# Experts' gate and up weights with eight consecutive feature rows on a partition

## The chip, the cores and the metric

The kernel runs on one core of a Trainium2 chip. The core has five engines that run side by side: TensorE (PE, with its weight loads shown apart as PEld), VectorE (DVE), ScalarE (ACT), GpSimd (POOL) and SyncE (SP), and 16 DMA engines that carry all transfers. The metric is the device time of one execution in microseconds. All times below are of the kernel before the change.

## What is computed

Two blocks work on 256 tokens of 1024 features, in float32. The first block (attention, a pool mixer and a gated feed-forward) is not touched. The second block has two layers, and each does this:

```python
mix = hybrid_mixer(x, ...)
x = layer_norm(ALPHA * x + mix, ln1_g[l], ln1_b[l])
ffn = grouped_moe(x, router_w, router_bias, w_gate[l], w_up[l], w_down[l])
x = layer_norm(ALPHA * x + ffn, ln2_g[l], ln2_b[l])
```

The experts' part, with 16 experts of 512 inner features, two of them chosen for a token:

```python
aff = jax.nn.sigmoid((xt @ router_w).astype(jnp.float32))
...
gates = jnp.sum(jax.nn.one_hot(e_idx, N_EXPERTS, dtype=jnp.float32) * wts[..., None], axis=1)
hg = jnp.einsum('nd,edf->nef', xt, w_gate)
hu = jnp.einsum('nd,edf->nef', xt, w_up)
act = jax.nn.silu(hg) * hu * gates[:, :, None].astype(hg.dtype)
out = jnp.einsum('nef,efd->nd', act, w_down)
```

The contraction of `w_gate` and `w_up` runs over the 1024 features of a token. Their order in it is free, as long as weights and tokens have the same one.

## The kernel before

The 1024 features are cut into 8 tiles of 128 (`KD`). A contraction over features puts 128 of them on the partitions at a time and adds up 8 such steps in PSUM. The tile framework orders the instructions of each engine by itself, within their dependencies and by its own estimate of when they can start, so the order of the code is not always the order on the engine.

At the start of the program SP issues the loads of x and of the first layer's weights `w_in`. POOL issues small loads on its own queue: in the code first `at` (constants of the attention) and the parts of `bw` (lines 266 to 275), then the tiles of the pool `const` (`upb`, `cr`, `rbias`, `rw`, lines 276 to 284).

In a layer of the second block the output projection leaves its sums in PSUM, 128 tokens a half. The first layer norm writes them as `z` (line 1075), tokens on partitions and the 1024 features next to each other, as 8 blocks of 128. TensorE transposes `z`, and `affine` (line 1083) scales the transposed tiles by the norm's gain and bias, a scalar for each partition, which gives `xp`. The router takes `xp`. Beside that, POOL splits `z` into a high and a low part, `zh` and `zl` (lines 1120 to 1122), since a product with both parts keeps float32's accuracy. VectorE works out the chosen experts in a chain of small steps (lines 1123 to 1151), and each token's slot of an expert (`sid`, line 1160); `residual` (line 1096) puts the scaled `xp` into PSUM, where the experts add to it.

`slots` (line 1165) turns the slots into a matrix `G` of zeros and ones for four experts. `gather` (line 1185) multiplies `zh` and `zl` with `G`, feature tile by feature tile, and `affine` scales the result to `xg`: features on partitions, 64 slots for each of four experts. `gate_up` (line 1201) contracts `xg` with the gate or the up weights of a pair of experts: feature tile `4 * h + k` of `xg` meets `W[..., k]` of half `h`. Each matmul takes 64 slots and 512 columns, in float32; the trace shows two records for each. The down products follow, and `combine` (line 1224) adds the outputs to the tokens. The stage runs over 8 pairs of experts.

`Experts.pump` (line 713) issues the weights on SP's queue in the order of their use, in pieces of 1 MB: four feature tiles of a gate or up matrix, or two of the four tiles of a down matrix. The first gate pieces and those of the last two pairs come in halves (lines 722 to 728 and 736 to 751). A piece goes to a ring or to tiles that earlier work has left, and SP waits until the space is free. Gate and up go by `"(k p) f -> p k f"`: a partition gets one row of 512 numbers from each feature tile, 2 KB at a time. Down goes by `"(p k) f -> p k f"`: a partition gets two consecutive rows of 1024 numbers, 8 KB in one run.

Of the kernel before, what the change touches and what calls it, by code (L numbers as in the profile page):

```python
# [10 lines left out]
F32 = mybir.dt.float32  # L11
# [10 lines left out]
KD = D // 128  # L22
# [8 lines left out]
# Scores of a head: 128 queries with 128 keys, then 128 queries with all 256 keys.  # L31
# [3 lines left out]
def body(tc, a, out, dbg=None, upto=None):  # L35
# [9 lines left out]
    def A(name, shape=(128, 512)):  # L45
        """One bank of PSUM."""
        return psum.tile(list(shape), F32, tag="A", name=name, bufs=4)

    def H(name, shape=(128, 2, 512)):
        """Two banks of PSUM."""  # L50
        return psum.tile(list(shape), F32, tag="H", name=name, bufs=2)
# [16 lines left out]
    def pin(i):  # L68
        """Keeps an instruction in the order of the program on its engine."""
        return tc.keep_in_program_order(i)  # L70

# [12 lines left out]
    def split(raw, shape=(1024,), eng=None, tile_=hl8, scale=1.0):  # L84
        """raw = hi + lo, both exact in float32r."""
        t = tile_("hl", F32R, (128, 2, 1024))
        n = int(np.prod(shape))
        hi, lo = (t[:, i, 0:n] for i in range(2))
        if len(shape) == 2:
            hi, lo = (v.rearrange("p (a b) -> p a b", b=shape[1]) for v in (hi, lo))  # L90
        if raw is not None:
            se.activation(hi, raw, AF.Copy, scale=scale)  # L92
            HI["lo"] = lo_of(lo, raw, hi, eng)
        return hi, lo

    HI = {}
    def keep_warm(n, dst):
        """Without work the clock of the tensor engine falls to half: this bridges a wait."""
        for _ in range(n):
            te.transpose(dst, ident, ident)  # L100
# [3 lines left out]
    def after(i, col):  # L104
        """behind[i] = 1, once col is there: keeps an operation scaled by it behind col."""
        ve.tensor_scalar(behind[:, i:i + 1], col, 1.0, 1.0, op0=ALU.max, op1=ALU.min)

    def table(func, col):
        """Loads the table of a function, once col is there."""
        se.activation(warm[:, 1:2], col, func, scale=0.0, bias=epsc[0:1, 0:1])  # L110

# [29 lines left out]
    # rows of per-channel vectors, put on partitions by the tensor engine  # L141
# [57 lines left out]
    def pre(seq, i, ahead=2, scale=1.0):  # L199
        """Keeps the splits of the units in seq up to i + ahead issued."""  # L200
        for name, j in seq[pre.done:i + ahead + 1]:
            HI[name, j] = split(W[name][:, j], scale=scale)
        pre.done = max(pre.done, min(i + ahead + 1, len(seq)))
# [47 lines left out]
    class at:  # L251
        """What only the attention needs (and the convolution, at first): a tile for each layer."""
# [27 lines left out]
    # the last rows come a second time, as the router takes 32 columns at once and drops 16  # L280
# [12 lines left out]
    def tm_mm(c, acc, k):  # L293
# [3 lines left out]
        if c == k == 0:  # L297
            # the low part of the weights comes last
            for i, (x, w) in enumerate(((hh, wh), (hl, wh), (hh, wl))):
                for tt in range(2):  # L300
                    for h in range(2):
                        tm_mm.last = mm(acc[tt][h], x[:, 0, tt * 128:(tt + 1) * 128], w[:, h * 512:h * 512 + 512], i == 0, False)
            return
# [15 lines left out]
    for k in range(KD):  # L319
# [4 lines left out]
        if k == 3:  # L324
            # statistics of the norm, and the vectors that come later
# [52 lines left out]
    def softmax_heads(S, n_, scale, nscale, values, hi, lo):  # L378
        """Scores of two heads, a bank each, to attention outputs with features on partitions."""
# [74 lines left out]
    def fm_out(units, xh, xl, evac, then=None):  # L454
        """8 feature tiles [128, 256] in 4 banks; units: (weight name, row) per contraction tile."""
# [101 lines left out]
    def up_split(i, ss=(0, 1)):  # L557
        """hi and lo of the weights of tile pair i, gate and value."""
        c, o = divmod(i, 2)
        for s in ss:  # L560
            UP[i, s] = split(W[f"up{c}{s}"][:, :, o * 128:o * 128 + 128], (KD, 128))
# [9 lines left out]
    def row_of(cols):  # L571
        """Two columns [128, 1] of tokens as a row [128, 256] on every partition."""
# [33 lines left out]
    def up_pair(i):  # L606
# [6 lines left out]
        # the first waits for the last of h2  # L613
# [59 lines left out]
    # =============================== second block ===============================  # L673
# [29 lines left out]
    class Experts:  # L703
        """The experts' weights in 8 KB pieces, which go around the ring and the tiles
        that the attention has left."""

        def __init__(self, l):
            self.l, self.n, self.final = l, 0, []
            self.todo = [(p, m, h, e) for p in range(8) for m in range(3) for h in range(2) for e in range(2)]
            # the second half of the first gate's contraction goes to the ring, which has space later  # L710
            self.todo[2:10] = self.todo[4:10] + self.todo[2:4]

        def pump(self, n):
            while self.n < min(n, len(self.todo)):
# [4 lines left out]
                if p == m == 0:  # L719
                    # the first in halves, as the space of the first halves is needed early  # L720
                    self.n += 2
                    for b in range(2):
                        for e in range(2):
                            t = ring.tile([128, 2, 512], F32, name=name)
                            c0 = 512 * h + 256 * b
                            sy.dma_start(t, a["w_gate_2"][self.l, e, c0:c0 + 256].rearrange("(k p) f -> p k f", p=128))
# [8 lines left out]
                src = src.rearrange("(k p) f -> p k f" if m < 2 else "(p k) f -> p k f", p=128)[:, shape[1] * h:shape[1] * (h + 1)]  # L735
                if p < 6:
                    sy.dma_start(t, src)
                elif p == 7 and m == 2:
                    # all first halves of the columns, then all second
# [5 lines left out]
                elif e:  # L745
                    # in halves, so that the products don't wait long for any and little is left after the last
# [9 lines left out]
    def transpose_rows(z, evac, one_bank):  # L756
        """z(k, tt) [128 tokens, 128 features] -> features on partitions."""
# [32 lines left out]
    def layer(l, xT, xh, xl, general=False):  # L790
# [7 lines left out]
        # high, high and low part of a head's index queries below each other, high, low and high of the keys  # L798
# [3 lines left out]
        # high and low part of a head's queries below each other, the keys' high parts twice and their low parts  # L802
        dq2, dk2 = act("dq2", F32R, (128, 8, T)), t2("dk2", (128, 2, T), F32R)
        nh, nl = act("nh", F32R), act("nl", F32R)
        # queries and keys, a head a column block: 64 rows without position, then the rope
        # q_r * cos, q_r * sin on the side of the queries, the rotated key and its swapped halves on the keys'
# [27 lines left out]
        def proj(i, ahead=1):  # L834
            for q in range(ahead + 1):
                prep(i + q)
            if i not in PS:
                # the first two side by side, as x comes slower than one of them takes it
# [49 lines left out]
        def index_scores(g):  # L888
# [4 lines left out]
            for b, h in enumerate(hs):  # L893
                # all keys for both halves of the queries; the second half's scores go over the first's of later keys
# [30 lines left out]
        def latent_stats():  # L925
            """1 / rms of the latent queries and keys, a token a partition; that of the keys as a row too."""
# [44 lines left out]
        def queries(g):  # L971
            """Two heads: columns without position, and the rope's columns twice."""
# [21 lines left out]
        def dsa_pair(j):  # L994
            S = H("sc")
            for tt, (c, n) in enumerate(SPAN):
                t_ = slice(tt * 128, tt * 128 + 128)
                for i in range(2):
                    h = 2 * j + i
                    r = slice(32 * (h % 4), 32 * (h % 4) + 2)  # L1000
                    # all keys for both halves of the queries; the second half's scores go over the first's of later keys
# [81 lines left out]
        def affine(dst, src, k, eng):  # L1083
            g, b = V(f"ln1g{l}", k), V(f"ln1b{l}", k)
# [11 lines left out]
        def residual():  # L1096
            """The scaled residual in PSUM, where the experts add to it."""
# [22 lines left out]
        for tt in range(2):  # L1120
            ge.tensor_copy(zh[:, tt], z[:, tt])
            lo_of(zl[:, tt], z[:, tt], zh[:, tt], ge)
        ve.tensor_tensor(out=bia, in0=aff, in1=rbias[:, None, :].to_broadcast([128, 2, 16]), op=ALU.add)
        b4 = R[:, 1].rearrange("p (g e) -> p g e", e=4)
        # the two best of a group of four sum to the best of: both of a pair, the better of each pair
# [33 lines left out]
        # a token's slot of an expert counts from 1, and 0 is none  # L1159
        ve.scalar_tensor_tensor(out=sid, in0=pk, scalar=1.0, in1=sel, op0=ALU.add, op1=ALU.mult)  # L1160

# [1 line left out]
        XG, GS, Y, S6 = {}, {}, {}, {}  # L1163

        def slots(q):
            """Which token has which of the 64 slots of four experts, and the slots' gates."""
# [18 lines left out]
        def gather(q, bs=range(4)):  # L1185
            """The tokens of four experts, features on partitions, 64 slots each."""
# [4 lines left out]
            for b in bs:  # L1191
# [6 lines left out]
                for i in range(2):  # L1198
                    affine(xg[:, 2 * b + i], pg[:, i], 2 * b + i, (se, ve)[b % 2])
# [16 lines left out]
        def slot_rows(p):  # L1216
            """The slots of two experts as rows."""
# [13 lines left out]
        def dense_experts():  # L1231
            """Every expert over every token."""
# [176 lines left out]
    if dbg is None:  # L1409
        # More tokens for an expert than it has slots: the second block again, in the general way.  # L1410
# [14 lines left out]
def constants():  # L1425
# [24 lines left out]
    # rows 0 to 31: which of the key's 32 features comes first, which second  # L1450
# [50 lines left out]
```

## Time and profile before

| | |
|---|---|
| device time, median of 3 runs | 1088.08 us (1087.83 to 1089.63) |
| span of the profiled execution, first to last instruction | 1082.4 us |
| PE busy | 1034.8 us (96%) |
| DVE busy | 540.0 us (50%) |
| ACT busy | 427.3 us (39%) |
| POOL busy | 80.4 us (7%) |
| DMA | 295.08 MB, mean 273 GB/s |
| loads of the experts' gate weights | 40 of 1024 KB, 48 of 512 KB |
| loads of the experts' up weights | 48 of 1024 KB, 32 of 512 KB |
| loads of the experts' down weights | 48 of 1024 KB, 32 of 512 KB |

The span runs from the first to the last instruction of the one execution that was profiled; the device time has what lies around it as well, 5.7 us at the median. A busy share says how long an engine worked, not whether others waited for it. That is read from the waits and from the order of time.

### The profile page before, as it was taken

To read this page: it belongs to the slowest core of one execution; us is meant where nothing else is said; L and a number is where in the kernel's file an instruction comes from. 1 tells how busy PE (TensorE), PEld (TensorE's weight loads), DVE (VectorE), ACT (ScalarE), POOL (GpSimd) and SP (SyncE) were. 2 spreads that over 40 slices of the span, in tenths; PEclk is the share of its full clock that TensorE was granted. 3 is DMA by queue.
4 is the path that set the end of the run, shared out by engine and by line. 5 is a ranking of instruction groups with operands and counts; after the bars stand their busy time and mean duration, and the time that the engine had idled before them with its cause. 6 is when DMAs were issued, how large, how long until landed. Compare 5 with 4: busy or idle time off the path is not lost.

```text
span 1082.4 us, 16579 instructions
## 1 busy us (share of the span) xinstructions
PE 1034.8 (96%) x6732; PEld 738.8 (68%) x6732; DVE 540.0 (50%) x1026; ACT 427.3 (39%) x795; POOL 80.4 (7%) x70
## 2 busy tenths in 40 slices
PE   7999999999999999999999999989999999999994
PEld 5889999999999999765343444368977534343431
DVE  3875578977777689753110111058985402011103
ACT  4766547755554565542110111156654302011111
POOL 3200021000000130010000000044000200000001
PEclk9999999999999999999999999999999999999997
DMA  9752555765443244978999999955297899999993
GB/s 320 307 183 79 208 185 173 256 203 184 156 143 142 83 159 141 352 279 311 397 394 394 396 399 395 377 201 197 79 338 283 315 381 394 398 399 400 395 387 121
DMA packets 131484, 295.08 MB, mean 273 GB/s; under 512 B 5754, under 2 KB 34744, under 8 KB 125128
## 3 DMA queue, kind: packets, MB, share of 16 engines
q1 hardware_dynamic: 130328, 290.58, 72.8%
q0 software_dynamic: 768, 2.84, 0.8%
q8 instruction: 55, 0.90, 0.3%
q10 hardware_dynamic: 304, 0.53, 0.1%
q14 instruction: 29, 0.24, 0.1%
HBM read 291.82 MB, written 2.10 MB: 272 GB/s over the span
## 4 chain that ended last, share of the span: by engine, by line
PE 79%; DVE 11%; DMA 4%; ACT 3%; issue 2%; SPq 0%; POOL 0%; DVEq 0%; ACTq 0%; POOLq 0%
PE gu L74 19%; PE up L74 12%; PE pd L74 10%; PE fm L74 7%; PE yT L74 5%; PE wo L74 5%; PE sc L74 4%; PE tm L74 4%; PE prj L74 3%; PE pg L74 3%; PE sum L74 3%; DVE hl L82 2%; PE sc L399 1%; DMA e<-in_w_down_dram 1%; DMA in<-in_w_in_dram 1%
## 5 line engine op out<-in xcount | busy, mean ns | idle before, releaser
L74 PE MATMUL gu<-e,xg 128*64 128x512 f32 x1024 | 224.2, 593 | 0.0
L74 PEld LDWEIGHTS gu<-e,xg 128*64 128x64 f32 x1024 | 72.3, 137 | 140.1 <-issue 131.5
L74 PE MATMUL up<-h2h,hl 128*128 128x256 f32 x704 | 130.5, 283 | 0.0
L1295 DVE SCALAR_TENSOR_TENSOR sg<-gu,gcol,sg 128x512 f32<-128x512 f32 x16 | 12.0, 751 | 227.5 <-PE gu L74 162.7
L74 PE MATMUL pd<-e,aT 128*64 128x512 f32 x512 | 115.9, 596 | 4.7 <-ACT aT L1305 2.7
L74 PEld LDWEIGHTS up<-h2h,hl 128*128 128x128 f32 x704 | 111.4, 192 | 0.0
L74 PE MATMUL up<-h2l,hl 128*128 128x256 f32 x352 | 99.7, 283 | 0.1
L74 PEld LDWEIGHTS pd<-e,aT 128*64 128x64 f32 x512 | 35.5, 137 | 73.5 <-issue 64.6
L74 PEld LDWEIGHTS up<-h2l,hl 128*128 128x128 f32 x352 | 67.6, 192 | 0.3 <-DVE h2l L515 0.3
L74 PE MATMUL yT<-ac,hl 128*128 128x256 f32 x528 | 67.0, 283 | 0.1
L74 PEld LDWEIGHTS yT<-ac,hl 128*128 128x128 f32 x528 | 64.9, 192 | 0.3 <-ACT ac L635 0.3
L82 DVE TENSOR_TENSOR hl<-up,hl 128x1024 fp32r<-128x1024 f32 x44 | 53.8, 1225 | 19.5 <-ACT hl L92 19.4
L1288 ACT ACTIVATE sg<-gu 128x512 f32<-128x512 f32 x16 | 9.6, 597 | 128.4 <-PE gu L74 128.4
L92 ACT ACTIVATE hl<-up 128x1024 fp32r<-128x1024 f32 x44 | 46.1, 1052 | 33.9 <-PE up L74 28.4
L1323 ACT ACTIVATE y<-pd 128x512 fp32r<-128x512 f32 x32 | 18.2, 597 | 104.1 <-PE pd L74 78.9
L82 DVE TENSOR_TENSOR y<-pd,y 128x512 fp32r<-128x512 f32 x32 | 21.3, 687 | 62.6 <-ACT y L1323 62.5
L74 PE MATMUL fm<-hh,hl 128*128 128x256 f32 x256 | 49.2, 288 | 0.9 <-ACT vu L316 0.9
L74 PE MATMUL tm<-hl,hh 128*128 128x512 f32 x128 | 41.6, 407 | 4.2 <-ACT hl L92 2.4
L1088 DVE TENSOR_SCALAR xg<-pg,vec 128x256 f32<-128x256 f32 x32 | 15.9, 538 | 59.4 <-PE sum L74 44.2
L82 DVE TENSOR_TENSOR hl<-in,hl 128x1024 fp32r<-128x1024 f32 x32 | 38.3, 1220 | 13.9 <-ACT hl L92 13.7
L1222 ACT ACTIVATE GT<-pgt 128x256 fp32r<-128x256 f32 x16 | 6.2, 384 | 95.7 <-PE pgt L1220 95.7
L74 PE MATMUL prj<-xhn,hl 128*128 128x256 f32 x208 | 40.2, 287 | 3.8 <-DVE iq L82 2.6
(354 smaller groups left out, 2052.4 us busy)
## 6 DMA issues: line engine op xcount, KB each, us to landing
e<-in_w_up_dram SPq DMA_DIRECT2D x48, 1024.0 KB
e<-in_w_down_dram SPq DMA_DIRECT2D x48, 1024.0 KB
e<-in_w_gate_dram SPq DMA_DIRECT2D x40, 1024.0 KB
e<-in_w_gate_dram SPq DMA_DIRECT2D x48, 512.0 KB
up<-in_w_up_dram SPq DMA_DIRECT2D x22, 1024.0 KB
e<-in_w_up_dram SPq DMA_DIRECT2D x32, 512.0 KB
e<-in_w_down_dram SPq DMA_DIRECT2D x32, 512.0 KB
in<-in_w_in_dram SPq DMA_DIRECT2D x15, 1024.0 KB
```

The source lines that it names most:

```text
L74: return te.matmul(o, lhsT=l, rhs=r, start=start, stop=stop, skip_group_check=True)
L82: return (eng or ve).tensor_tensor(out=dst, in0=src, in1=hi.bitcast(F32), op=ALU.subtract)
L92: se.activation(hi, raw, AF.Copy, scale=scale)
L399: te.transpose(S[:, i, 128 * b:128 * b + 128], P[:, i, 128 * b:128 * b + 128], ident)
L1088: ve.tensor_scalar(dst, src, g, b, op0=ALU.mult, op1=ALU.add)
L1222: se.activation(GTs[p], pt, AF.Copy)
L1288: se.activation(sg, psg, AF.Silu)
L1295: ve.scalar_tensor_tensor(out=sg, in0=psu, scalar=gcol[:, p:p + 1], in1=sg, op0=ALU.mult, op1=ALU.mult)
L1323: se.activation(h_, pd[c], AF.Copy)
```

## The change

The gate and up weights are loaded as the down weights are: a partition takes eight consecutive feature rows of an expert, four in each half `h`, so 8 KB in one run for a full piece, and 4 KB for a half piece. Feature `8 * p + k` stands on partition `p` in step `k`, where it was feature `128 * k + p`. The gathered tokens must have the same order. So `zh` and `zl` are made from a view of `z` in which neighbouring elements of a row are 8 elements apart, and are written without gaps. `affine` in `gather` takes its gain and bias from a new constant tile `lnx`, which holds them in the new order; four small loads on POOL's queue fill it, each with 32 bytes for a partition. All other users of `z` and `xp` stay as they are. Comments are dropped in the new file, which is left out here.

```diff
@@ -277,13 +277,18 @@
     rbias = cload("rbias", (128, 16), a["router_bias_2"].partition_broadcast(128))
...
+    lnx = const.tile([128, 2, 2, KD], F32, name="lnx")
+    for l in range(2):
+        for i, n in enumerate(("ln1_g_2", "ln1_b_2")):
+            ge.dma_start(lnx[:, l, i], a[n][l].rearrange("(p k) -> p k", p=128))
+
     rw = const.tile([128, (KD + 1) * 16], F32, name="rw")
...
@@ -717,13 +722,13 @@
                             t = ring.tile([128, 2, 512], F32, name=name)
-                            c0 = 512 * h + 256 * b
-                            sy.dma_start(t, a["w_gate_2"][self.l, e, c0:c0 + 256].rearrange("(k p) f -> p k f", p=128))
+                            c0 = 4 * h + 2 * b
+                            sy.dma_start(t, a["w_gate_2"][self.l, e].rearrange("(p k) f -> p k f", p=128)[:, c0:c0 + 2])
...
@@ -732,18 +737,18 @@
                 src = a[("w_gate_2", "w_up_2", "w_down_2")[m]][self.l, 2 * p + e]
-                src = src.rearrange("(k p) f -> p k f" if m < 2 else "(p k) f -> p k f", p=128)[:, shape[1] * h:shape[1] * (h + 1)]
+                src = src.rearrange("(p k) f -> p k f", p=128)[:, shape[1] * h:shape[1] * (h + 1)]
...
@@ -1080,8 +1085,8 @@
-        def affine(dst, src, k, eng):
-            g, b = V(f"ln1g{l}", k), V(f"ln1b{l}", k)
+        def affine(dst, src, k, eng, by_rows=False):
+            g, b = (lnx[:, l, i, k:k + 1] for i in range(2)) if by_rows else (V(f"ln1g{l}", k), V(f"ln1b{l}", k))
...
@@ -1118,11 +1123,13 @@
         for tt in range(2):
-            ge.tensor_copy(zh[:, tt], z[:, tt])
-            lo_of(zl[:, tt], z[:, tt], zh[:, tt], ge)
...
+            zk = z[:, tt].rearrange("t k p -> t (k p)").rearrange("t (p k) -> t k p", k=KD)
+            ge.tensor_copy(zh[:, tt], zk)
+            lo_of(zl[:, tt], zk, zh[:, tt], ge)
...
@@ -1196,7 +1203,7 @@
-                    affine(xg[:, 2 * b + i], pg[:, i], 2 * b + i, (se, ve)[b % 2])
+                    affine(xg[:, 2 * b + i], pg[:, i], 2 * b + i, (se, ve)[b % 2], True)
```

## Rows read from the trace of the kernel before

**Rows 1.** The page: its span, the shares of the chain, the DMA packets.

```profile
span 1082.4 us, 16579 instructions
...
DMA packets 131484, 295.08 MB, mean 273 GB/s; under 512 B 5754, under 2 KB 34744, under 8 KB 125128
...
PE 79%; DVE 11%; DMA 4%; ACT 3%; issue 2%; SPq 0%; POOL 0%; DVEq 0%; ACTq 0%; POOLq 0%
```

**Rows 2.** Windows: length, busy (x instructions) by engine, PEclk, DMA share, GB/s.

```profile
615.00:620.00 5.00, 5.00 (x26) 1.60 (x24) 0.00 (x0) 0.28 (x1) 0.00 (x0) 1.00 1.05 386
...
625.00:630.00 5.00, 5.00 (x26) 1.58 (x22) 0.01 (x1) 0.60 (x1) 0.00 (x0) 1.00 1.04 422
```

**Rows 3.** Waits, 490 to 720 us: total, times, longest (PE, then PEld).

```profile
PE pact L1303 <- DVE sg L1295: 1.8, 3, 0.7
...
PEld gu L74 <- DMA e<-in_w_down_dram: 0.9, 3, 0.3
```

**Rows 4.** Timeline (start, length, what, [idle before]): PE, then SP's queue.

```profile
630.86 13.90 PE L74 MATMUL gu<-e,xg 128*64 128x512 f32 x64
...
702.46 5.37 PE L74 MATMUL pd<-e,aT 128*64 128x512 f32 x24 [0.69 <-ACT aT L1305]
...
683.44 10.23 SPq L744 DMA_DIRECT2D e<-in_w_down_dram  x8
```

**Rows 5.** Timeline of POOL ahead of the first layer's experts.

```profile
484.00 1.04 POOL L1121 CAST zh<-z 128x1024 fp32r<-128x1024 f32 x1 [1.64 <-ACT z L786]
485.00 4.66 POOL L82 TENSOR_TENSOR zl<-z,zh 128x1024 fp32r<-128x1024 f32 x2
```

**Rows 6.** Timeline of DVE and PE ahead of the experts of both layers.

```profile
489.20 0.51 DVE L1123 TENSOR_TENSOR R<-R,rbias 128x32 f32<-128x32 f32 x1 [1.02 <-ACT R L1119]
...
492.70 0.76 DVE L1169 TENSOR_TENSOR G<-cr,R 128x256 fp32r<-128x256 f32 x2
...
493.27 0.36 PE L74 MATMUL pg<-G,zh 128*128 128x256 f32 x1 [0.51 <-DVE G L1169]
...
846.65 0.51 DVE L1123 TENSOR_TENSOR R<-R,rbias 128x32 f32<-128x32 f32 x1 [1.02 <-ACT R L1119]
```

**Rows 7.** Timeline of POOL and DVE in the first block, 45 to 52 us.

```profile
45.47 5.95 POOL L354 TENSOR_TENSOR qk<-qk,bw 128x512 f32<-128x512 f32 x4 [35.08 <-DVE qk L352]
...
48.90 1.37 DVE L359 TENSOR_TENSOR rot<-qk,bw 128x128 f32<-128x128 f32 x1 [2.44 <-POOL qk L354]
...
51.49 0.28 DVE L361 TENSOR_TENSOR rot<-qk,bw 128x128 f32<-128x128 f32 x1
```

**Rows 8.** Timeline of POOL: a cast of 512 columns.

```profile
377.13 0.61 POOL L854 CAST iq<-iq 32x512 fp32r<-32x512 f32 x1 [0.46 <-ACT iq L851]
```

**Rows 9.** The start: timeline of POOL, ACT and PE, then windows as in rows 2.

```profile
5.15 0.55 POOL L284 DMA_DIRECT2D rw<-in_router_w_dram  x1
5.69 0.53 POOL L256 DMA_DIRECT2D at<-in_c_att_dram  x1
...
17.06 2.00 ACT L92 ACTIVATE hl<-in 128x1024 fp32r<-128x1024 f32 x2 [5.09 <-DMA in<-in_w_in_dram]
...
18.16 0.50 PE L74 MATMUL tm<-hl,hh 128*128 128x512 f32 x1 [2.44 <-ACT hl L92]
...
10.00:15.00 5.00, 4.24 (x22) 3.19 (x21) 1.62 (x2) 1.51 (x2) 0.39 (x1) 1.00 1.09 306
15.00:20.00 5.00, 1.80 (x8) 0.93 (x7) 1.77 (x3) 2.73 (x4) 0.00 (x0) 1.00 0.93 348
20.00:25.00 5.00, 5.00 (x16) 3.96 (x15) 2.46 (x4) 2.37 (x3) 0.00 (x0) 0.66 1.02 398
```

**Rows 10.** Windows, as in rows 2, around a pause of TensorE.

```profile
730.00:735.00 5.00, 2.92 (x26) 2.74 (x24) 4.84 (x6) 3.56 (x7) 4.52 (x4) 1.00 0.69 236
735.00:740.00 5.00, 4.44 (x36) 4.23 (x36) 4.81 (x9) 3.83 (x9) 1.27 (x1) 1.00 0.00 0
```

**Rows 11.** Waits of SP's queue: total, times, longest.

```profile
SPq L737 <- POOL zl L82: 9.0, 2, 4.5
```

More of the change, by code (lines that the diff above doesn't have):

```diff
@@ L251, in body @@
     class at:
+        pass
     def attention_tile(eng):
```

## The prediction

> **What bounds the kernel now.** I read the page first. The chain that ended last is 79% TensorE [rows 1], so the question for every part of the change is whether TensorE waits for it. The change aims at the experts' gate and up weights, so I went on to the two expert stages (about 493 to 714 us and 851 to 1069 us). There the transfers look like a second bound. While only gate and up pieces are under way the 16 DMA engines are full (share 1.05) at 386 GB/s; while down pieces, whose runs are already 8 KB, are under way they move 422 GB/s [rows 2]. But the waits say who is late. In 490 to 720 us TensorE's longest kind of wait is 1.8 us in three pieces, for VectorE's product before the transposes; waits of the weight loads that are put down to a transfer are 0.3 us each [rows 3], no more than the gaps between any two of those loads. The timeline agrees: the 64 gate and up matmuls of a pair take 13.90 us without a break, 217 ns each. The last down pieces of the layer have been issued by 693.67, and TensorE begins on them at 702.46, where it waits 0.69 us for ScalarE's aT and not for a weight [rows 4]. So the expert stage is bound by TensorE, and the transfers arrive in time with some microseconds to spare.
>
> Just ahead of each stage it is another engine that is late. On POOL zh of the second token half runs from 484.00, then both zl from 485.00 to 489.66 [rows 5]. VectorE's first step of the router's choice, L1123, starts at 489.20 and takes 0.51 us for 32 columns; it ends at 489.71, right after POOL. From there the choice runs without a pause to G at 492.70, and the gather's first matmul, at 493.27, has waited 0.51 us for G. The second layer repeats it at 846.65 [rows 6]. That POOL holds VectorE up here is seen elsewhere: while POOL runs the four products of L354 (45.47 to 51.42), VectorE's L359 takes 1.37 us, and the like step after it, L361, 0.28 us [rows 7]. Both read two operands from SBUF, as L1123 does. So the end of zl is on the path that sets the end, with no slack left.
>
> **The change part by part.** *The loads.* By the table of loads above, 40 + 48 = 88 gate and up pieces of 1 MB go from 512 runs to 128, and 48 + 32 = 80 of 0.5 MB from 256 to 128: 88 x 384 + 80 x 128 = 44,032 packets fewer of 131,484. That consecutive rows do become one packet is shown by the down weights: 48 pieces x 128 = 6,144 of the 131,484 - 125,128 = 6,356 packets that have 8 KB or more [rows 1]. At 422 instead of 386 GB/s [rows 2], the 67.1 MB of gate and up of a layer take 159.0 us of transfer instead of 173.9: 14.9 us less. All of it lies beside TensorE's own work. Its value is between -0.9 us a layer, were the wait of [rows 3] all due to transfers, and 0; I take 0, because those waits are as short as the ordinary gap. If that cover were gone the most to win would be the 14.9 us. What comes earlier is only the next layer's loads, and the first work after the experts waits for their sums.
>
> *zh and zl.* As many POOL operations as before, but z is read at a step of 8 elements, 32 bytes. The trace has no POOL operation with such a step. Below, nothing: the same number of elements is read (a gain has no reason). Above: each operation gets longer by what a whole second operand costs, 2.33 - 1.04 = 1.29 us for 1024 columns [rows 5]. Between these the nearest price is one more pass of reading: a cast of 1024 columns takes 1.04 us, one of 512 takes 0.61 [rows 5, 8], so 1024 columns read once are worth 2 x 0.43 = 0.86 us. I take that, as if every stepped element cost two reads. On the path stand three operations after 484.00 (zh of the second half, zl twice); zh of the first half, at 481, has time. 3 x 0.86 = 2.6 us a layer (0 to 3.9), and +5.2 us for both (0 to 7.7). At most one short VectorE step slips in between two POOL operations, so I subtract nothing. Nothing later gives it back, as TensorE is the bound of the stage that follows. SP is queued behind the same operation: its next expert load waits 4.5 us a layer for zl, which frees z [rows 11], and would wait 7.1. Those are loads of the second pair, not read before the first pair is done, and faster transfers make it up; I cost it at nothing. If that cover failed, 2.6 us more a layer would come late.
>
> [...]
>
> *Four small loads for lnx on POOL's queue.* Four more issues of 0.53 to 0.55 us each, 2.2 us. In the code "at" and "bw" stand ahead of the router's constants, on the queue behind them: rw is issued at 5.15, at only at 5.69 [rows 9]. lnx is a constant of the same kind, so I expect it ahead of "at", which with the parts of bw then starts some 2 us later. POOL's next operation is at 45.47 [rows 7], so the wait on the queue is covered by over 30 us; without that it would be 2.2 us. But something else is moved: "at" and bw compete with the first layer's weights. Between 10 and 15 us the engines move 306 GB/s, between 20 and 25 us 398; ScalarE waits 5.09 us for a piece of w_in until 17.06, and TensorE 2.44 us until 18.16 [rows 9]. If "at" comes later, w_in can come earlier, and that wait goes: -2.4 us. Against it, small runs slow the engines: if 10 to 15 us lost 5 x (1 - 306/398) = 1.2 us to some eleven small loads, four more cost 0.4 us; I allow +1.0. Between -2.4 and +1.0 I take the middle, -0.7.
>
> *The rest*: gather has the same matmuls on contiguous slices of zh and zl, the affine step takes its two scalars from another tile, the residual still uses xp, and the two weights of a contraction step stay matched. Nothing.
>
> **The sum.** 0 + 5.2 - 0.7 = +4.5 us, against the profiled span of 1082.4 us [rows 1]: 1086.9. The median of the runs shown is 5.7 us above that span, so 1092.6 us. For one measurement of this kernel, 0.2% (2.2 us) is about what can be told from no change.
>
> **Rivals.**
> *The clock falls in the longer pause.* TensorE would stand idle some 3 us between the rank and the gather. In 15 to 20 us it was busy 1.80 of 5 us, and the granted clock of 20 to 25 us was 0.66, part of it at the lower level; that costs 5 x 0.34 = 1.7 us [rows 9]. In 730 to 735 us it was busy 2.92 of 5, and the clock stayed at 1.00 [rows 10]. The new pause lies between these. Price: 1.7 us in one layer or 3.4 in both, 1094.3 to 1096.0.
> *The step is free.* POOL reads 32-byte steps as fast as neighbours; then only the start moves: 1087.4 (1085.7 to 1089.1). For it: nothing in the trace shows a dear step. Against it: a second read stream does cost 1.29 us, so this engine's time follows its reads.
> *Faster, by the start.* The wait before 18.16 goes (2.4 us), and with it the slow clock after it (1.7 us): -4.1 us, 1084.0. It decides over the other side only where zh and zl cost under 0.95 us a layer (4.1 - 1.9 = 2.2); with the cost I expect, the sum is +1.1.
> *Faster, by the loads.* The experts wait for transfers after all: up to 2 x 14.9 us, 1058 us. [rows 3, 4] speak against it. If on the other hand the runs didn't merge, the loads would stay as they are and the forecast with them.
>
> **How the numbers follow.** Forecast (step paid, clock holds) 0.55, 1092.6; its own range, with zh and zl at 2.0 to 3.9 us a layer and the start at -2.4 to +1.0, is 1089.7 to 1096.8, and a quarter of it lies within 0.2%. Clock falls 0.15; step free 0.18; faster by the start 0.09; faster by the loads 0.03. Faster: 0.12. Within 0.2%: 0.13 of the forecast and most of the free step, 0.28. Slower: 0.60. The range goes from 1085.5, which takes in the free step, to 1097.5, which takes in a lost clock with my own POOL price.
>
> **What would show it.** zh at about 1.9 us and each zl at about 3.2; L1123 ending just after POOL, near 492.3 if the start hasn't moved; the first gather matmul some 2.6 us later after the last transpose of z; gate and up stretches at over 410 GB/s; some 87,700 packets; the matmuls of a pair still at 13.9 us. Wrong, if zh stays at 1.04 us, if TensorE's pairs come closer together, or if the start moves by more than its wait of 2.44 us.

## The result and the profile after

| | kernel before | changed kernel |
|---|---|---|
| median of the runs of the first comparison | 1088.04 us | 1094.43 us |
| ratio, with its 95% interval | | 1.0062 (1.0040 to 1.0083) |
| median of a second comparison on one chip | 1087.78 us | 1092.25 us, ratio 1.0040 (1.0026 to 1.0055) |
| span of the profiled execution | 1082.4 us | 1088.9 us |

The change makes the kernel slower by about 0.5%; both intervals lie above 1. The forecast was 1092.6 us, slower. How much of that was for the right reasons is the matter of what follows. Each of these executions takes 1.8 us more than its span.

The page of the changed kernel, against [rows 1]: span, packets, shares of the chain.

```profile
span 1088.9 us, 16583 instructions
...
DMA packets 87581, 295.11 MB, mean 271 GB/s; under 512 B 5882, under 2 KB 34872, under 8 KB 69960
...
PE 75%; DVE 11%; DMA 6%; ACT 4%; issue 3%; SPq 0%; POOL 0%; ACTq 0%; DVEq 0%; POOLq 0%
```

The consecutive rows did merge: the page has 43,903 packets fewer. Windows of the expert stage (as in [rows 2]), and a timeline row of the gate and up matmuls of one pair (start, length, what), against [rows 4]:

```profile
617.00:622.00 5.00, 5.00 (x26) 1.72 (x24) 0.00 (x0) 0.60 (x1) 0.00 (x0) 1.00 1.01 418
...
633.91 13.90 PE L74 MATMUL gu<-e,xg 128*64 128x512 f32 x64
```

The stretch that moved 386 GB/s now moves 418, and the 64 matmuls take 13.90 us as before. The transfers got faster and nobody was waiting for them.

Now the place ahead of the first layer's experts: timelines of POOL, VectorE and TensorE, against [rows 5, 6].

```profile
480.88 2.05 POOL L1128 CAST zh<-z 128x1024 fp32r<-128x1024 f32 x1 [65.59 <-PE wo L74]
483.83 2.06 POOL L1128 CAST zh<-z 128x1024 fp32r<-128x1024 f32 x1 [0.90 <-ACT z L791]
485.85 5.66 POOL L82 TENSOR_TENSOR zl<-z,zh 128x1024 fp32r<-128x1024 f32 x2
...
482.52 0.43 DVE L790 SCALAR_TENSOR_TENSOR mv<-mv 128x1 f32<-128x1 f32 x1
...
489.03 2.53 DVE L1130 TENSOR_TENSOR R<-R,rbias 128x32 f32<-128x32 f32 x1 [1.02 <-ACT R L1124]
...
494.06 0.22 PE L74 MATMUL rank<-selb,upb 128*128 128x16 bf16 x3 [2.52 <-DVE selb L1158]
...
495.11 0.55 PE L74 MATMUL pg<-G,zh 128*128 128x256 f32 x1 [0.47 <-DVE G L1176]
495.46 0.42 PE L74 MATMUL pg<-G,zl 128*128 128x256 f32 x1
```

zh takes 2.06 us where it took 1.04, each zl 2.83 where it took 2.33. L1130 (L1123 before) starts at 489.03 and ends at 491.56, right behind POOL's end at 491.51. TensorE stands still for 2.52 us ahead of the rank, where it was 0.51. Another row was not foreseen: the small step L790 of the second half's norm takes 0.43 us, where the same step took 0.16. It ends when zh of the first half does, at 482.93, and z of the second half comes 0.3 us late.

What the pause does to the clock, in windows of 2 us (PEclk is the third number from the end):

```profile
492.00:494.00 2.00, 0.00 (x0) 0.00 (x0) 1.90 (x13) 0.00 (x0) 0.00 (x0) 1.00 0.78 180
494.00:496.00 2.00, 1.47 (x9) 1.27 (x9) 1.55 (x8) 0.00 (x0) 0.00 (x0) 0.61 0.82 340
496.00:498.00 2.00, 2.00 (x12) 2.00 (x12) 0.05 (x1) 0.75 (x2) 0.00 (x0) 0.54 0.01 4
```

Behind this pause of 2.52 us the granted clock falls to its lower level (0.50 from 495.0 to 497.5 us, so 0.61 and 0.54 in the two windows that hold the gather): the gather's matmuls start 0.21 us apart instead of 0.12. The second layer shows the same behind its pause of 2.50 us (0.50 from 857 to 859 us).

Laid side by side, TensorE's instructions of the two profiles give the ledger. Up to the first of these layer norms the changed kernel leads by about 0.5 us. At the rank it is 1.85 us behind (492.21 against 494.06): 2.34 us lost to POOL. At the first gate matmul it is 3.05 behind (495.40 against 498.45): 1.21 us more, to the clock. Nothing changes until the second layer, where the rank is 5.36 behind and the gate 6.83, so 2.31 and 1.47 us. The span ends 6.5 us later.

### The profile page after: what moved, and what is told of

Read it like the earlier page. It is cut to its first block, busy times and chain, and to the rows that moved or that the text cites. A ratio compares the mean times of both kernels' runs of the same rounds, so it can differ in the third digit from the quotient of the medians.

```text
span 1088.9 us, 16583 instructions
## 1 busy us (share of the span) xinstructions
PE 1036.6 (95%) x6732; PEld 739.9 (68%) x6732; DVE 544.5 (50%) x1026; ACT 427.5 (39%) x795; POOL 88.4 (8%) x74
## 4 chain that ended last, share of the span: by engine, by line
PE 75%; DVE 11%; DMA 6%; ACT 4%; issue 3%; SPq 0%; POOL 0%; ACTq 0%; DVEq 0%; POOLq 0%
PE gu L74 17%; PE up L74 11%; PE pd L74 9%; PE fm L74 7%; PE yT L74 5%; PE wo L74 5%; PE sc L74 4%; PE pg L74 3%; PE prj L74 3%; PE sum L74 3%; DVE hl L82 2%; DMA e<-in_w_down_dram 2%; DMA in<-in_w_in_dram 2%; PE tm L74 2%; PE sc L404 1%
## 5 line engine op out<-in xcount | busy, mean ns | idle before, releaser
L1093 DVE TENSOR_SCALAR xg<-pg,lnx 128x256 f32<-128x256 f32 x32 | 15.9, 538 | 59.3 <-PE sum L74 44.2
```

Of the source, the lines that this page charges most:

```text
L1093: ve.tensor_scalar(dst, src, g, b, op0=ALU.mult, op1=ALU.add)
```

## The experiments

Theories that stood against each other: the loss comes from POOL's stepped reads and what follows from them, or it comes with the loads, or with the four small loads at the start. Ratios are to the kernel before in the same comparison.

**The loads alone.** The changed kernel without its other two parts:

```
-    zk = z[:, tt].rearrange("t k p -> t (k p)").rearrange("t (p k) -> t k p", k=KD)
-    ge.tensor_copy(zh[:, tt], zk)
-    lo_of(zl[:, tt], zk, zh[:, tt], ge)
+    ge.tensor_copy(zh[:, tt], z[:, tt])
+    lo_of(zl[:, tt], z[:, tt], zh[:, tt], ge)
     (no lnx; the affine step reads the old columns)
```

> The weights' loads as changed (8 KB runs), but zh and zl read z in order again, the layer norm's vectors come from the old columns, and the four new loads of vectors are left out. The gathered features then meet the wrong rows of the gate and up weights, so the values are not the reference's; the work and its sizes are. Theory (all of the loss comes from POOL's stepped reads and the low clock behind them, and the faster transfers are worth nothing, as TensorE does not wait for them): 1087.8 to 1088.2 us, gather's first matmul at 493.3 us as before, each gate/up pair at 13.9 us. Rival (the longer runs themselves cost, or the faster transfers disturb another engine): 1090 or more. Other rival (they gain, hidden in the changed kernel by the loss): under 1087.

Measured: 1087.90 us beside 1087.33, ratio 1.0005 (0.9990 to 1.0020). The expert stage moves 415 GB/s and the pair's matmuls take 13.90 us. No effect of the long runs shows, in either direction: the interval is -1.1 to +2.2 us. In its profile TensorE is 0.4 us ahead of the kernel before at 60 us, and still 0.4 us ahead at 580 us, well into the expert stage.

**The step alone.** The kernel before, with zh and zl reading z at 32 bytes.

```
-    ge.tensor_copy(zh[:, tt], z[:, tt])
-    lo_of(zl[:, tt], z[:, tt], zh[:, tt], ge)
+    zk = z[:, tt].rearrange("t k p -> t (k p)").rearrange("t (p k) -> t k p", k=KD)
+    ge.tensor_copy(zh[:, tt], zk)
+    lo_of(zl[:, tt], zk, zh[:, tt], ge)
```

> The kernel before with one edit: zh and zl read z with the step of 32 bytes. The weights keep their old order, so the gathered features meet the wrong rows; the work and its sizes are those of the kernel before. Theory: the whole loss appears, with the 0.5 us of the start missing: 1088.0 + 0.3 + 2.0 + 1.0 (layer 1) + 0.3 + 2.0 + 1.5 (layer 2) = about 1095 us; the biased scores end right behind POOL, 2 us later than before, and the clock falls in the pause ahead of the gather. Rival (loss is with the loads): 1088 to 1090.

Measured: 1093.49 us beside 1087.33, ratio 1.0059 (1.0037 to 1.0081). VectorE and TensorE in its timeline:

```profile
492.42 2.52 DVE L1124 TENSOR_TENSOR R<-R,rbias 128x32 f32<-128x32 f32 x1 [1.02 <-ACT R L1119]
...
497.43 0.23 PE L74 MATMUL rank<-selb,upb 128*128 128x16 bf16 x3 [2.50 <-DVE selb L1152]
```

The step alone brings a loss as large as the whole change's, about 6 us (4.0 to 8.8), with the old order of the weights. 1.5 us less than expected is within the spread of these few runs.

**The pause bridged.** The changed kernel, with work for TensorE in the pause:

```
+    total = residual()
+    with tc.issue_after(residual.last.ins):
+        for _ in range(18):
+            warm_last = te.transpose(pk[:, 1], ident, ident)
     (the rank's three matmuls behind warm_last)
```

> The changed kernel, with 18 transposes of the identity on TensorE between the residual's products and the rank's, which fill the pause of 2.52 us ahead of the rank (18 x 0.13 = 2.3 us). Theory: TensorE is never idle for more than 0.5 us there, the granted clock stays at its upper level through the gather, and 1.05 us (layer 1) and 1.45 us (layer 2) come back: 1094.4 - 2.5 = 1091.9 us. POOL's share, 2.0 and 0.3 us in each layer, stays. Rival (the clock falls anyway, or the low clock overlaps waits and costs nothing): 1094 to 1095.

Measured: 1089.61 us, ratio 1.0024 (1.0009 to 1.0038), against the 1.0040 and 1.0062 of the changed kernel. TensorE, then the same windows as above:

```profile
491.76 2.13 PE L1164 MATMUL rank<-ident 128*128 128x128 f32 x18
494.22 0.22 PE L74 MATMUL rank<-selb,upb 128*128 128x16 bf16 x3 [0.33 <-DVE selb L1158]
...
494.00:496.00 2.00, 0.94 (x9) 0.88 (x9) 1.58 (x7) 0.00 (x0) 0.00 (x0) 1.00 0.83 348
496.00:498.00 2.00, 2.00 (x18) 1.65 (x19) 0.74 (x3) 1.02 (x2) 0.00 (x0) 1.00 0.04 16
```

The clock holds, and POOL and VectorE are as late as in the changed kernel. From the rank to the first gate matmul TensorE takes 3.17 and 3.18 us in the two layers; the changed kernel took 4.39 and 4.65, the kernel before 3.19 and 3.18. So the clock's part of the loss, 1.2 and 1.5 us, is shown in the profile. What is left in TensorE's ledger is 2.34 and 2.29 us, POOL's part. In the times the size is less sure: this kernel is 2.3 us behind the kernel before of its own comparison, the changed kernel was 4.5 behind in the second and 6.4 in the first, so 2.2 or 4.1 us come back, where 2.5 were reckoned, and the intervals of this run and of the second comparison overlap.

**The changed kernel again.** No edit.

> The changed kernel once more, beside the others on one chip. Its profiled run was 1090.65 us, its other runs 1094 to 1095, and the variant with the bridged pause came to 1089.6 us, 4.8 below the changed kernel's median where 2.5 had been reckoned from the two low-clock stretches of the profiled run. Theory: an ordinary run of the changed kernel has one or two low-clock stretches more, 1.5 us each, behind the pauses of 0.96 us ahead of the down product at about 594 and 955 us, as runs of the kernels without the step have too; the low clock ahead of the gather makes them no likelier. Then the median stays at 1094 and a profile at 1093 or more shows four such stretches. Rival: the runs differ elsewhere (transfers, or the time outside of the span).

Measured: 1092.25 us. Its profile, at 1092.17, has the two low-clock stretches ahead of the experts and one more, but not where I had put it: it stands at 182 us, in the feed-forward, and TensorE falls 1.5 us further behind there.

```profile
180.00:182.00 2.00, 1.82 (x15) 1.64 (x15) 1.49 (x3) 1.77 (x3) 0.00 (x0) 0.97 0.35 135
182.00:184.00 2.00, 2.00 (x11) 2.00 (x10) 1.88 (x3) 1.97 (x3) 0.00 (x0) 0.50 0.00 0
```

So executions differ by low-clock stretches, at about 1.5 us each, in places that all of these kernels have. The profile of the loads alone has two, at 592 and 951 us, behind pauses of 0.96 us (0.58 and 0.56 in the two windows from 592 to 596 us); the profiled kernel before has the same pauses (0.96 and 0.99 us) and no low clock there (1.00 in these stretches). Among the runs of the kernel before, one with a mean granted clock of 0.993 has a span of 1081.6 us, one with 0.988 a span of 1088.5. Why a given run has such a stretch is open.

**The four small loads alone.** The kernel before, with the loads and nothing that reads them:

```
+    lnx = const.tile([128, 2, 2, KD], F32, name="lnx")
+    for l in range(2):
+        for i, n in enumerate(("ln1_g_2", "ln1_b_2")):
+            ge.dma_start(lnx[:, l, i], a[n][l].rearrange("(p k) -> p k", p=128))
```

> The kernel before with one addition: the four small loads of the layer norms' vectors on POOL's queue ahead of the router's weights and the attention's tile; nothing reads them. Theory: as in the changed kernel, TensorE's wait of 2.4 us for the first norm's parts at 16 us and the low clock from 20 us are gone, later waits give most of that back, and 0.4 to 1.0 us stay: about 1086.7 us beside 1087.3 for the kernel before. Rival (the start of the changed kernel differs by chance, run by run): the wait of about 2 us at 16 us is there again, time as before. Other rival (the loads' 4096 packets delay the input weights): 1088 or more.

Measured: 1085.28 us beside 1087.78, ratio 0.9975 (0.9964 to 0.9985). A gain of 2.5 us, more than expected. The loads are 128 packets on POOL's queue (752 in the first 30 us, 624 before), not 4096. POOL's queue, and windows of the start, against [rows 9]:

```profile
8.69 0.54 POOL L256 DMA_DIRECT2D at<-in_c_att_dram  x1 [0.41 <-DMA cr<-in_c_route_dram]
...
10.00:15.00 5.00, 4.24 (x23) 3.32 (x22) 1.62 (x2) 2.12 (x3) 2.88 (x5) 1.00 1.03 354
15.00:20.00 5.00, 4.30 (x19) 3.23 (x18) 3.23 (x4) 2.13 (x4) 0.00 (x0) 1.00 1.02 344
20.00:25.00 5.00, 3.92 (x18) 2.93 (x17) 2.75 (x3) 2.37 (x3) 0.00 (x0) 1.00 1.02 393
...
25.01 1.06 ACT L92 ACTIVATE hl<-in 128x1024 fp32r<-128x1024 f32 x1 [2.19 <-DMA in<-in_w_in_dram]
```

The last row is ScalarE's last wait for a piece of w_in in this stretch; in the kernel before it reads:

```profile
25.38 1.06 ACT L92 ACTIVATE hl<-in 128x1024 fp32r<-128x1024 f32 x1 [0.47 <-DMA in<-in_w_in_dram]
```

"at" starts at 8.69 instead of 5.69, TensorE is busy 4.30 us of 15 to 20 instead of 1.80, and the clock of 20 to 25 stays at 1.00 instead of 0.66. But little of that lasts: TensorE leads by 4.3 us at 24 us and by 0.4 us at 40. The piece of w_in that ScalarE waits for until 25.01 came at 25.38 before, so nearly as late, and from there ScalarE works in both kernels without a wait for another load until past 40 us.

So in this profile the start is worth 0.4 us of the 2.5. The rest goes with the clock of the whole run: the mean granted clock has a median of 0.994 in the ten runs with the four small loads and of 0.990 in the fourteen runs of the kernel before. At the same mean clock the spans are no shorter (at 0.993, 1084.5 us with the loads and 1083.5 without; at 0.991, 1086.4 and 1085.7). At about 1.5 us each, 2 us is one or two low-clock stretches fewer in a run. Only one of these ten runs was profiled, the slowest, so where the stretches went, and why, is open.

**The queue held up without loads.** The kernel before, with POOL busy for 2.7 us ahead of "at":

```
+    for _ in range(5):
+        ge.tensor_scalar(alphaI, ident, ALPHA, None, op0=ALU.mult)
     attention_tile(ge)
```

> The kernel before, with five repeats of one small POOL operation (0.54 us each, the same values written again) among the issues on POOL's queue ahead of the attention's tile, in place of the four small loads. Theory (the small loads help only by making the 1.5 MB of the attention's and the pool's constants start 2.7 us later, so that the input weights come first): the wait at 16 us and the low clock behind it are gone, and the time is that with the four loads, 1085.3 us beside 1087.5 for the kernel before. Rival (it is the loads themselves, or their packets): 1087.5 and the wait of 2.4 us as before.

Measured: 1084.18 us beside 1085.44, ratio 0.9989 (0.9972 to 1.0006). The wait at 16 us and the low clock behind it are gone here too, so a later "at" is enough for that. Here it starts at 9.87, so it is held back by 1.2 us more than with the loads. And one wait of 3.1 us has come at 27 us, with a low clock of its own (the profile's mean is 0.993, as in the kernel before), and the interval holds no change. That a delay gives the 2.5 us is not shown.

**The step on TensorE.** zh and zl in order again, the step in the gather's weight loads:

```
-    mm(pg[:, i], zh[:, tt, k], G[:, tt], tt == i == 0, False)
-    mm(pg[:, i], zl[:, tt, k], G[:, tt], False, tt == 1)
+    h_, l_ = (v[:, tt].rearrange("t k p -> t (k p)")[:, k:1024:KD] for v in (zh, zl))
+    mm(pg[:, i], h_, G[:, tt], tt == i == 0, False)
+    mm(pg[:, i], l_, G[:, tt], False, tt == 1)
```

> The changed kernel, but zh and zl are made from z in order, as before, and the step of 32 bytes is put into TensorE's weight loads of the gather (every eighth column of zh and zl as the stationary operand). Theory: POOL takes 1.04 and 2.33 us for each again, so the biased scores are back at 489.5 us, the pause is 0.5 us again and the clock stays up: 1088.0 - 0.5 = 1087.5 us. Rival (a stepped weight load costs TensorE as it cost POOL: the first gather's 16 loads lie on the path, and if each matmul there takes 0.21 us in place of 0.12 that is 1.4 us for the first half of a gather and 5.8 us for a layer's 4 gathers at most): 1090 to 1099.

Measured: 1119.91 us, ratio 1.0307 (1.0285 to 1.0330). The rows of tile pg (ns: least, median, most), first of the changed kernel, then of this one:

```profile
L74 PEld LDWEIGHTS pg<-G,zl x128: 187/192/338, 495.2 to 1024.6; 128*128 128x128 f32 x128
L74 PE MATMUL pg<-G,zl x128: 278/283/420, 495.5 to 1024.7; 128*128 128x256 f32 x128
```

```profile
L74 PEld LDWEIGHTS pg<-G,zl x128: 328/339/345, 493.3 to 1052.3; 128*128 128x128 f32 x128
L74 PE MATMUL pg<-G,zl x128: 398/405/457, 493.4 to 1052.5; 128*128 128x256 f32 x128
```

A stepped weight load takes 339 ns instead of 192, and the matmuls start 0.247 us apart instead of 0.12: 256 of them x 0.127 = 32 us as an estimate, beside 32.6 measured against the kernel before. The agreement is closer than it should be, since this profile has five low-clock stretches from 599 us on as well (mean granted clock 0.988). My expectation had 5.8 us a layer at most: it reckoned with 0.21 us for each matmul, and with 64 of a layer's 128. POOL's part went as the theory says: zh 1.04 us again, zl 2.33, and the pause 0.50.

**POOL's work in two parts.** The half that the gather needs first, then the other:

```
+    def z_parts(h):
+        ks = slice(4 * h, 4 * h + 4)
+        ...
+    z_parts(0)
 ...
     slots(0)
+    with tc.issue_after(slots.last.ins):
+        z_parts(1)
```

> The changed kernel with POOL's stepped work in two parts: zh and zl of the features that the first half of the gather takes (1.03 + 1.03 + 1.42 + 1.42 us) as before, those of the second half after the matrix G of the first four experts. Theory (POOL's operations keep VectorE's operations on SBUF waiting, so what counts is when POOL is done, not that the step is there): the first parts end at about 487.7 us, ahead of the scores at 489.0; the biased scores take 0.2 us, the pause ahead of the rank is 0.5 us or less, the gather begins 0.3 us earlier than in the kernel before, and the second parts (4.9 us from 492.8) end before the gather's second half at 498.5: about 1087.3 - 0.5 - 0.6 = 1086.2 us. Rival (the step costs wherever it lies: the second parts hold up VectorE's work for the gates and the gather's evictions, or the loads that wait for z's space): 1089 or more.

Measured: 1096.08 us, ratio 1.0068 (1.0044 to 1.0092). The second part was not held back: nothing in its data made it wait, and it followed the first at once. So the run tests something else, POOL busy for 2 us longer:

```profile
488.39 2.17 POOL L1130 CAST zh<-z 128x512 fp32r<-128x512 f32 x2
490.52 3.00 POOL L82 TENSOR_TENSOR zl<-z,zh 128x512 fp32r<-128x512 f32 x2
...
489.58 1.03 DVE L1135 TENSOR_TENSOR R<-R,rbias 128x32 f32<-128x32 f32 x1 [1.02 <-ACT R L1124]
490.65 1.43 DVE L1140 TENSOR_TENSOR R<-R 128x16 f32<-128x16 f32 x1
492.00 1.55 DVE L1141 TENSOR_TENSOR R<-R 128x16 f32<-128x16 f32 x1
493.47 0.28 DVE L1157 TENSOR_TENSOR cmp<-R 128x128 f32<-128x128 f32 x1
```

One VectorE step with two operands from SBUF gets through between two POOL operations, and the chain runs freely once POOL is done, at 493.52. The end of POOL's work sets the rank. The same kernel with 7 transposes in the pause of 0.96 us ahead of the fourth pair's down product:

> As the run with POOL's work in two parts, and 7 transposes of the identity on TensorE in the pause of 0.96 us ahead of the fourth pair's down product of each layer, behind which the clock fell to its lower level in several profiles. Theory: the stretches at about 591 and 950 us go, 1.5 us each in the runs that had them: 1 to 3 us below the run without the transposes, 1083.5 to 1085 us. Rival (the transposes end late and delay the down product, or the stretches come elsewhere): no difference.

Measured: 1093.05 us, ratio 1.0050 (1.0032 to 1.0068). Its profile has no low clock at 592 or 951 us (mean 0.992, 0.989 without the transposes), and 3.0 us less than the run without the transposes, but the few runs of each leave the size open.

**The second part really held back,** by a factor 1 that VectorE writes after G:

```
-    pin(ge.tensor_copy(zh[:, tt, ks], zk[tt]))
+    pin(ge.tensor_scalar(zh[:, tt, ks], zk[tt], behind[:, 3:4], None, op0=ALU.mult))
 ...
+    after(3, GS[0][:, 1, 255:256].bitcast(F32))
+    z_parts(1)
```

> The changed kernel, with POOL's stepped work in two parts of which the second now really waits: its two reads of z are scaled by a 1 that VectorE writes once G of the first four experts is there, and VectorE takes the gather's first evictions ahead of the gates; and the 7 transposes ahead of the fourth pair's down product. (In the earlier run in two parts the second part followed the first at once.) Theory (POOL's operations keep VectorE waiting, and only the end of the part ahead of the scores matters): the first parts end at about 488, the biased scores take 0.2 us at 489.0, the pause ahead of the rank is 0.5 us or less, the clock stays up, the second parts run at 493 to 498.5: then the changed kernel has lost its loss and keeps the start, 1083 us, or 0.997 of the kernel before. Rival (the step costs wherever it lies, as the second parts hold up the gates, the gather's second half or the loads into z's space): 1087 or more.

Measured: 1099.66 us, ratio 1.0128 (1.0105 to 1.0151): slower still. VectorE and TensorE ahead of the experts:

```profile
488.98 0.19 DVE L1138 TENSOR_TENSOR R<-R,rbias 128x32 f32<-128x32 f32 x1 [1.02 <-ACT R L1124]
...
491.67 0.22 PE L74 MATMUL rank<-selb,upb 128*128 128x16 bf16 x3 [0.18 <-DVE selb L1166]
...
500.32 0.99 DVE L1093 TENSOR_SCALAR xg<-pg,lnx 128x256 f32<-128x256 f32 x2 [5.19 <-POOL zl L82]
...
500.94 5.45 PE L74 MATMUL gu<-e,xg 128*64 128x512 f32 x16 [6.01 <-ACT xg L1091]
```

The first half of the theory is shown: with POOL done in time the biased scores take 0.19 us and the pause is 0.18, shorter than in the kernel before. The second half is not. The evictions into xg wait for the last zl, though they read nothing that POOL writes; most likely xg takes the space that z gives up when zl is done, as both come from one pool of ten tiles in the code. So here a 6 us wait took the place of the 2.5 us one. Whether the step could be hidden with other space for xg was not tried.

**What the runs point to.** The kernel before, with the four small loads and the 7 transposes, and none of the new order:

> The kernel before with the two things that the other runs point to and none of the new order: the four small loads ahead on POOL's queue (nothing reads them), and 7 transposes of the identity on TensorE in the pause of 0.96 us ahead of the fourth pair's down product of each layer. Theory: no wait of 2 us at 16 us and no low clock behind it, and no low clock at 591 and 950 us, which many runs of the kernel before have, 1.5 us each: 1083 to 1084.5 us, under the kernel before and under the changed kernel. Rival (the low clock comes elsewhere, or the transposes delay the down product): as with the loads alone, 1085.3.

Measured: 1083.31 us beside 1085.44, ratio 0.9975 (0.9959 to 0.9991). It is faster than the kernel before, and so than the changed one. Against the small loads alone the ratio is the same, so what the transposes add is not shown.

## Why the forecast held, point by point

Two terms were wrong in opposite directions and nearly cancelled, so that the sum came so close is in part luck. By the runs, the step costs 6.2 us (4.0 to 8.8; the ledger of the profiles has 4.6 for POOL and 2.7 for the clock, 7.3 in all), the four small loads give back 2.5, and of the faster weight loads nothing shows. 6.2 - 2.5 = 3.7 us, or 4.8 with the ledger's numbers, beside 4.5 and 6.4 in the two comparisons. The two first profiles alone, in which the start gives only 0.5 us, make it 7.3 - 0.5 = 6.8, and their spans differ by 6.5. The forecast had 5.2 - 0.7 = 4.5: near in its sum, with the clock left out and without most of the gain that goes with the four small loads.

- *The bound.* Right. The 14.9 us of transfer a layer lay wholly beside TensorE's work, as the waits of [rows 3] had said, although [rows 2] showed full DMA engines. The rival by the loads is excluded: by its interval the run with the weights' loads alone gains 1.1 us at most.
- *zh and zl.* The path was right (POOL, L1123, G, gather), and the sum was near: 2.6 us a layer forecast, 2.34 measured. Its parts were not. I charged each operation 0.86 us, one pass of reading. The cast paid 1.02, the subtraction 0.50 (2.33 to 2.83), so the three operations on the path paid 2.0 us.
- *"zh of the first half, at 481, has time."* Wrong, by 0.3 us a layer. It had time on its own path, but it kept VectorE's L790 waiting, and with it z of the second half. I had looked for that blocking at one VectorE step only.
- *The clock.* The step that failed. I held the fall for unlikely (0.15), from a stretch in which TensorE was busy 2.92 of 5 us and kept its clock [rows 10]. The longest pause there is 2.08 us; here it was 2.52, and the clock fell in both layers of both profiles of the changed kernel, at 1.2 to 1.5 us each (I had 1.7). The run with the pause bridged shows that it was the pause. Its length alone does not decide, as the pauses of 0.96 us at 592 and 951 us show.
- *The start.* The wait of 2.44 us went as foreseen, and the low clock behind it, which I listed as a rival, with it: it begins at 19 to 20 us in all three profiles without the four small loads or a delay in their place (0.66, 0.77 and 0.50 in 20 to 25 us), and there in none of the nine with them (1.00 in 15 to 25 us of the changed kernel; one has a low clock at 31 us). The size at the start was near, -0.7 taken and -0.5 in the two first profiles at 48 us. The +1.0 us that I allowed for small runs did not show: with four more of them 10 to 15 us moves 352 GB/s in the changed kernel, where it was 306. The rival's 4.1 us is too much, since ScalarE gets the piece of w_in that sets the pace after 25 us hardly earlier. What failed is that I looked for the effect of the four small loads at the start alone: by the run with nothing else changed they give -2.5 us (-3.9 to -1.6), with a higher granted clock over the run. I had no term for that, and its cause is open.
- *From span to time.* I added 5.7 us, the distance of the median from the profiled span. 1.8 of it lies around the span in every run; the rest is most likely low-clock stretches that the profiled execution happened not to have (its mean granted clock is 0.993, the median of fourteen later runs 0.990). The conversion held all the same, since the changed kernel has such stretches too: its first median stands 5.5 us above its profiled span.
- *SP's wait for zl.* 6.5 us a layer, with 7.1 forecast; nobody waited for what is behind it. Packets, transfer rates and the pair's 13.90 us came as forecast.

## What to carry to other kernels

A layout that makes loads faster is worth nothing while the waits on those loads are no longer than ordinary gaps (0.3 us each here, and a ratio of 1.0005 for the loads alone), and the reorder that pays for it lands somewhere: ask which engine does it, and who is kept waiting while it runs, every small step on the other engine included. When a wait on TensorE's path grows from half a microsecond to two and a half, as here, price the clock with it, for the work behind the pause can run at the lower level (0.50 here, 1.2 and 1.5 us in the two layers). Ahead of a queue's large transfers even small loads are an edit of the order: here four of them were worth 2.5 us of the run, and the faster weight loads that the change was about nothing that shows.

## What the runs showed of the hardware

- POOL's step of 32 bytes doubles a cast of 1024 columns (1.04 to 2.06 us, kernel before and changed kernel) and adds a fifth to a subtraction with one stepped operand (2.33 to 2.83 us).
- A scaled copy with that step is dearer still: 2.07 us for 512 columns, where the stepped cast takes 1.12 (runs with POOL's work in two parts). No run has such a copy without the step.
- VectorE steps with two operands from SBUF wait for the POOL operation in progress (2.53 us for one of 0.19), while its evictions from PSUM, the four of L1093 in 1.90 us, run beside the same POOL work (two of them take 0.99 us where POOL is idle, at 498.64 us of the changed kernel).
- A weight load of TensorE with a step of 32 bytes takes 339 ns instead of 192, and the matmuls start 0.247 us apart instead of 0.12.
